# Seven block products in place of eight in sixteen FFN blocks of a decoder layer, and a down product by pairs

## The chip, the cores and the metric

One core of one Trainium2 chip runs one launch of the kernel. The metric is the time of a launch in microseconds (us), the median of three runs. Times in the trace are from one further execution, taken with the hardware profiler; durations of single instructions are in us or, where a view gives a mean, in ns. Engines are called PE (TensorE), DVE (VectorE), ACT (ScalarE), POOL (GpSimd) and SP (SyncE, which issues most loads).

## The reference, cut to what matters

One layer of a hybrid decoder, 1024 prompt tokens and 64 sample tokens (8 sequences of 8), all fp32. A token-mixing sub-layer (short convolution and three kinds of attention) comes first, then a dense SwiGLU FFN and a last RMSNorm:

```python
D_MODEL = 1024
D_FF = -(-8 * D_MODEL // (3 * 256)) * 256        # 2816

def swiglu(h, w_gate_up, w_down):
    gate, up = jnp.split(h @ w_gate_up, 2, axis=-1)
    return (jax.nn.silu(gate) * up) @ w_down
...
    x = x + gate1 * (mix @ w_out)
    x = x + gate2 * swiglu(rmsnorm(x, g_ffn) * (1 + scale2) + shift2, w_gate_up, w_down)
```

The change touches `swiglu` and a little of what stands behind it. The scales and gates are one column for all prompt tokens and one for each of the eight sample sequences.

## The kernel before

Activations lie with channels on the 128 partitions and the 1088 tokens along the free axis. `GRP` cuts the tokens into three groups of 366, 366 and 356 columns; the last holds the 64 sample tokens, so that 292 of its columns are prompt. The 2816 hidden channels are 22 FFN blocks of 128. A block needs 8 chunks of 128 input channels for its gate and 8 for its up product.

An fp32 product is made of three matmuls for each chunk (`mm3`, L197 to L204): every operand is held as a rounded half and the rest (hi and lo), and w_hi a_hi, w_hi a_lo and w_lo a_hi are added up in PSUM. A weight tile is 128x512 (four chunks); `load` (L93) brings it on SP's queue into one of five `wraw` buffers, and `halves` (L83) makes hi on ACT (L88) and lo on DVE (L89) into one of four `wsp` buffers. In an earlier part of the kernel every second L89 is on POOL (`state["sub"]`); in the FFN none is.

`gate_up` (L826) runs `gemm` twice: for the gate (two weight tiles; ACT takes Silu from PSUM into a row `u`, L829) and for the up product (two more; DVE multiplies `u` by PSUM, L833). `split_hid` then makes the halves of the hidden row, ACT L848 for hi and DVE L849 for lo. With three groups a block has 2 x 3 x 8 x 3 = 144 matmuls.

`down` (L851) multiplies hidden blocks by rows of w_down into PSUM; `add_gated` adds the result, times the gate, to the residual `x1` (DVE L760; for the third group L764 and L765 as well, for the sample tokens). `FF_GROUPS` says which blocks pass the down product together: blocks 0 to 3, then the pair (20, 21), then 4 to 7, 8 to 11, 12 to 15 and 16 to 19. For each of eight output chunks m and each token group a set of four blocks has 12 matmuls and one `add_gated`, a pair 6 and one.

Blocks 0 to 3 have groups 0 and 1 done ahead, under the attention of the sample tokens, and 20 and 21 have theirs done in front of the FFN. What the FFN itself starts with is group 2 of blocks 0 to 3 and their down product, group 2 of blocks 20 and 21 and the down product of that pair; then come the sixteen full blocks 4 to 19. The last set (16 to 19) passes the down product by other column groups, `LAST` (416, 416 and 256 columns), so that behind each of them `rstd` and the final norm follow: squares on ACT, their sums on DVE and POOL (L791), two small sets of matmuls (L794 and L798), a multiply per chunk on DVE (L970) or POOL (L968) and a store.

The order on each engine is set by the tile framework, which puts instructions in place by a timeline of its own, within what pools and buffers allow. Every engine then runs its row in order. PSUM has buffers under four tags, g (three in `gemm`), s, t and o; in the FFN of the kernel before only g is used until the last norm.

In the DRAM copies that go along with the FFN (cache outputs), `next_copy` issues one or two per block from ACT's queue.

## Time and profile before

| | us |
|---|---|
| median of three runs | 1426.48 (1424.07 to 1427.05) |
| the profiled execution, its own time | 1429.4 |
| its span, first to last instruction | 1427.6 |
| PE busy in the span | 1383.2 (97%) |
| DVE, ACT, POOL busy | 650.8, 529.3, 222.7 |
| the full blocks 4 to 19, first to last matmul of gate and up | about 835 to 1362 |
| last down product and last norm | 1363 to 1427.6 |

Busy times of PE are of matmuls whose ends are modelled, and which overlap; what one matmul costs is read from how many start in a stretch. The profiled execution took 2.9 us longer than the median, and sums are made against it.

### The profile page before, as it was taken

To read this page: it belongs to the slowest core of one execution; us is meant where nothing else is said; L and a number is where in the kernel's file an instruction comes from. 1 tells how busy PE (TensorE), PEld (TensorE's weight loads), DVE (VectorE), ACT (ScalarE), POOL (GpSimd) and SP (SyncE) were. 2 spreads that over 40 slices of the span, in tenths; PEclk is the share of its full clock that TensorE was granted. 3 is DMA by queue.
4 is the path that set the end of the run, shared out by engine and by line. 5 is a ranking of instruction groups with operands and counts; after the bars stand their busy time and mean duration, and the time that the engine had idled before them with its cause. 6 is when DMAs were issued, how large, how long until landed. Compare 5 with 4: busy or idle time off the path is not lost.

```text
span 1427.6 us, 23603 instructions
## 1 busy us (share of the span) xinstructions
PE 1383.2 (97%) x9289; PEld 1319.7 (92%) x9289; DVE 650.8 (46%) x1599; ACT 529.3 (37%) x1108; POOL 222.7 (16%) x284
## 2 busy tenths in 40 slices
PE   7999999999999999998999999999999999999996
PEld 5889999988898887888999999999999999999996
DVE  4457777255775326224554642242224222422145
ACT  5387765465654335322344312211221122112242
POOL 2143333233334220111110000000000000000023
PEclk9999999999999998999999999999999999999998
DMA  9342331352416679865444434723341332111103
GB/s 357 105 157 98 126 105 24 127 194 89 141 31 216 220 257 332 300 211 164 120 128 126 126 102 159 242 82 104 102 162 46 103 104 73 45 45 45 45 8 126
DMA packets 100799, 190.78 MB, mean 134 GB/s; under 512 B 14048, under 2 KB 51456, under 8 KB 100096
## 3 DMA queue, kind: packets, MB, share of 16 engines
q1 hardware_dynamic: 94112, 135.67, 29.8%
q10 hardware_dynamic: 6416, 53.55, 10.6%
q8 instruction: 73, 1.20, 0.3%
q14 instruction: 38, 0.31, 0.1%
q0 software_dynamic: 160, 0.04, 0.0%
HBM read 181.22 MB, written 59.23 MB: 168 GB/s over the span
## 4 chain that ended last, share of the span: by engine, by line
PE 88%; DMA 6%; DVE 2%; issue 2%; ACT 1%; POOL 1%; SPq 0%; ACTq 0%; POOLq 0%; DVEq 0%
PE ps_g L202 25%; PE ps_g L203 25%; PE ps_g L204 25%; PE ps_o L576 3%; PE ps_t L567 2%; DMA raw<-in_bv 2%; PE ps_s L525 1%; PE ps_g L178 1%; DMA wraw<-in_w_gu 1%; PE ps_s L526 1%; DMA raw<-in_bk 1%; DMA mraw<-in_wmod 1%; PE ps_s L658 1%; PE ps_o L692 1%; DMA wraw<-in_wmod 0%
## 5 line engine op out<-in xcount | busy, mean ns | idle before, releaser
L202 PE MATMUL ps_g<-act,wsp 128*128 128x366 f32 (+1 forms) x1704 | 568.4, 334 | 5.0 <-ACT wsp L88 2.6
L203 PE MATMUL ps_g<-act,wsp 128*128 128x366 f32 (+1 forms) x1704 | 565.8, 332 | 0.5 <-DVE act L614 0.5
L204 PE MATMUL ps_g<-act,wsp 128*128 128x366 f32 (+1 forms) x1704 | 564.3, 332 | 0.4 <-POOL wsp L89 0.4
L202 PEld LDWEIGHTS ps_g<-act,wsp 128*128 128x128 f32 x1704 | 323.6, 190 | 12.5 <-issue 5.5
L203 PEld LDWEIGHTS ps_g<-act,wsp 128*128 128x128 f32 x1704 | 323.8, 190 | 4.3 <-issue 2.8
L204 PEld LDWEIGHTS ps_g<-act,wsp 128*128 128x128 f32 x1704 | 322.9, 190 | 4.7 <-issue 3.3
L88 ACT ACTIVATE wsp<-wraw 128x512 fp32r<-128x512 f32 x228 | 143.1, 630 | 470.5 <-PE ps_g L204 314.5
L89 DVE TENSOR_TENSOR wsp<-wraw,wsp 128x512 fp32r<-128x512 f32 x190 | 134.4, 707 | 356.3 <-ACT wsp L88 353.5
L204 PE MATMUL ps_g<-hid,wsp 128*128 128x366 f32 (+3 forms) x416 | 136.5, 328 | 0.0
L203 PE MATMUL ps_g<-hid,wsp 128*128 128x366 f32 (+3 forms) x416 | 136.0, 327 | 0.0
L202 PE MATMUL ps_g<-hid,wsp 128*128 128x366 f32 (+3 forms) x416 | 135.6, 328 | 0.2 <-DVE ts L764 0.2
L791 POOL TENSOR_TENSOR lacc<-lacc,tmp 128x416 f32<-128x416 f32 x9 | 9.8, 1087 | 637.8 <-ACT tmp L790 637.3
L202 PEld LDWEIGHTS ps_g<-hid,wsp 128*128 128x128 f32 x416 | 78.1, 188 | 0.5 <-PE ps_g L204 0.5
L203 PEld LDWEIGHTS ps_g<-hid,wsp 128*128 128x128 f32 x416 | 78.2, 188 | 0.0
L204 PEld LDWEIGHTS ps_g<-hid,wsp 128*128 128x128 f32 x416 | 78.2, 188 | 0.0
L89 POOL TENSOR_TENSOR wsp<-wraw,wsp 128x512 fp32r<-128x512 f32 x38 | 49.6, 1306 | 166.5 <-ACT wsp L88 154.9
L539 ACT ACTIVATE Sb<-Sb,st 128x257 f32<-128x257 f32 (+5 forms) x96 | 60.6, 633 | 17.0 <-DVE st L531 15.0
L571 DVE TENSOR_TENSOR PT<-ps_t,PT 128x512 fp32r<-128x512 f32 (+1 forms) x84 | 52.2, 636 | 15.9 <-ACT PT L570 15.6
L576 PE MATMUL ps_o<-PT,Vt 128*128 128x256 f32 (+1 forms) x348 | 59.2, 288 | 0.0
L760 DVE SCALAR_TENSOR_TENSOR p_qc<-ps_g,MOD,p_qc 128x366 f32<-128x366 f32 (+3 forms) x63 | 36.0, 573 | 49.5 <-PE ps_g L204 49.2
L567 PE MATMUL ps_t<-ident,Sb 128*128 128x128 f32 x306 | 51.9, 283 | 5.9 <-DVE Sb L542 5.3
L576 PEld LDWEIGHTS ps_o<-PT,Vt 128*128 128x128 f32 x348 | 52.3, 195 | 5.1 <-issue 2.1
(319 smaller groups left out, 1604.3 us busy)
## 6 DMA issues: line engine op xcount, KB each, us to landing
wraw<-in_w_gu SPq DMA_DIRECT2D x112, 256.0 KB, 2.6
wraw<-in_wmod SPq DMA_DIRECT2D x64, 256.0 KB, 3.6
raw<-in_bk SPq DMA_DIRECT2D x30, 512.0 KB, 7.5
raw<-in_bv SPq DMA_DIRECT2D x30, 512.0 KB, 8.8
wraw<-in_w_dn SPq DMA_DIRECT2D x48, 256.0 KB, 2.7
out_bk_b<-in_bk ACTq DMA_DIRECT2D x12, 1016.0 KB, 8.8
wraw<-in_w_in SPq DMA_DIRECT2D x36, 256.0 KB, 3.1
mraw<-in_wmod SPq DMA_DIRECT2D x32, 256.0 KB, 5.7
```

What stands on the lines that cost most here:

```text
L88: S.activation(sp[:, 0, :], raw, AF.Copy)
L89: (V if not state["sub"] or state["n"] % state["sub"] else G).tensor_tensor(sp[:, 1, :], raw, sp[:, 0, :].bitcast(F32), op=OP.subtract)
L178: ins = PE.matmul(ps[32 * q:32 * q + 32, :256], lhsT=csil[:, 4 * hf + q, :], rhs=raws[2 * hf + q // 2][:, q % 2 * 256:q % 2 * 256 + 256], ...
L202: PE.matmul(ps[:, :n], lhsT=w_hi, rhs=a(0, ak), start=first and j == 0, stop=False)
L203: PE.matmul(ps[:, :n], lhsT=w_hi, rhs=a(1, ak), start=False, stop=False)
L204: PE.matmul(ps[:, :n], lhsT=w_lo, rhs=a(0, ak), start=False, stop=last and j == m - 1)
L525: PE.matmul(ps[:, :sn], lhsT=QH[:, qsl], rhs=KS[hd][:, kk], start=True, stop=False)
L539: S.activation(Sb[:, :ne], Sb[:, :ne], AF.Exp, scale=-1.0, bias=m, accum_out=st[:, 3:4])
L567: PE.transpose(pt[:, col:col + 128], Sb[:, (kb - k0) * 128:(kb - k0 + 1) * 128], ident)
L571: V.tensor_tensor(PT[:, 1, :col], pt[:, :col], PT[:, 0, :col].bitcast(F32), op=OP.subtract)
L576: PE.matmul(po[:, q0:q0 + w], lhsT=Vt[:, kb, hd].rearrange("p a b -> p (a b)"), rhs=PT[:, hl, c0:c0 + w], start=fresh, stop=ch is chunks[- ...
L760: ins = V.scalar_tensor_tensor(x1[m][:, c0:c0 + k], ps[:, :k], MOD[:, gate + m, 0:1], x1[m][:, c0:c0 + k], op0=OP.mult, op1=OP.add)
```

## The change

Sixteen full blocks (4 to 19) take the gate and up products of token groups 0 and 1 together. Seen as a 2x2 matter, the two halves of the input channels by the two products (gate, up) on the one side, and the two token groups by the two halves on the other, this is eight block products of 12 matmuls each. The new `gate_up_2x2` makes them from seven, in the form of Strassen and Winograd, of sums of weights and sums of activations. The third token group (356 columns) is done as before, with its four block products of 12.

- Weights: t1 to t4 are made on POOL, four `tensor_tensor` of 128x512 per block, into four `tw` buffers; `halves` runs on eight tiles per block (b11, t2, t3, b21, t1, t4, b22, b12) where it ran on four.
- Activations: `sums_step(k)` for k = 0 to 3 makes SA1 to SA4 once, among the third-group work of blocks 0 to 3. Each step has four POOL adds of 128x366 (`whole`: hi plus lo gives fp32), four DVE sums, four ACT copies and four DVE subtractions (`keep`). SA3 takes the place of `h2[1]` chunks 0 to 3.
- PSUM: products run under tags s and t, and three of them add to a bank that DVE or ACT has read before (`more`). Per block DVE adds PSUM to the rows `u2` and `u3` four times and into g1 once, and multiplies in SBUF for groups 0 and 1; ACT copies the first product to `u2` and takes Silu of g1 in SBUF.
- Down: `FF_GROUPS` has pairs for blocks 4 to 19, weights come as `w_d2`, `hid` has two buffers rather than five. The last pair (18, 19) alone is left for `LAST`, with four weight tiles and 144 matmuls where there were eight tiles and 288.
- Pools: tiles that are used only ahead of the FFN go to a pool `early`, closed before it. The FFN's pools have `reuse_waits="tile"`. Cache copies are issued once a block.

```diff
-FF_GROUPS = ((0, 4), (20, 2), (4, 4), (8, 4), (12, 4), (16, 4))
+FF_GROUPS = ((0, 4), (20, 2)) + tuple((f, 2) for f in range(4, 20, 2))
...
-            return ff.tile([128, 2, T], F32R, tag="hid", bufs=5, name="hid")
+            return ff.tile([128, 2, T], F32R, tag="hid", bufs=2, name="hid")
...
+        def whole(src, k):
+            t = tw()[:, :N2]
+            G.tensor_tensor(t, src[:, 0, k, :].bitcast(F32), src[:, 1, k, :].bitcast(F32), op=OP.add)
+            return t
...
+        def sums_step(k):
+
+            a21, a22, a11 = whole(h2[1], k), whole(h2[1], k + 4), whole(h2[0], k)
+            V.tensor_tensor(a22, a21, a22, op=OP.add)
+            keep(1, k, a22)
+            V.tensor_tensor(a21, a11, a21, op=OP.subtract)
+            keep(3, k, a21)
+            V.tensor_tensor(a11, a22, a11, op=OP.subtract)
+            keep(2, k, a11)
+            a12 = whole(h2[0], k + 4)
+            V.tensor_tensor(a12, a12, a11, op=OP.subtract)
+            keep(4, k, a12)
...
+        def gate_up_2x2(f, hh):
+            c2, n2 = GRP[2]
+            b11, b12, b22, b21 = [load(d["w_gu"][f, n, hf]) for n, hf in ((0, 0), (1, 0), (1, 1), (0, 1))]
+            t1, t2, t3, t4 = [tw() for _ in range(4)]
+            G.tensor_tensor(t1, b12, b11, op=OP.subtract)
+            G.tensor_tensor(t2, b22, t1, op=OP.subtract)
+            G.tensor_tensor(t3, b22, b12, op=OP.subtract)
+            G.tensor_tensor(t4, b21, t2, op=OP.subtract)
...
+            product(pa, w, lambda hl, k: h2[0][:, hl, k, :], True)
+            S.activation(u2, pa[:, :N2], AF.Copy)
+            third(pg, w, 0, True)
+            pb = ps_tile("t")
+            product(pb, wsel(halves(t2)), lambda hl, k: SA[2][:, hl, k, :], True)
+            V.tensor_tensor(u2, u2, pb[:, :N2], op=OP.add)
...
+            product(pd, wsel(halves(t4)), lambda hl, k: h2[1][:, hl, 4 + k, :], False)
+            V.tensor_tensor(g1, u2, pd[:, :N2], op=OP.add)
+            S.activation(g1, g1, AF.Silu)
+            V.tensor_tensor(g1, g1, u3, op=OP.mult)
+            split_hid(u, hh, N2, N2)
+            w = wsel(halves(b22))
+            product(pe, w, lambda hl, k: SA[4][:, hl, k, :], False)
+            V.tensor_tensor(u2, u2, pe[:, :N2], op=OP.add)
+            V.tensor_tensor(g0, g0, u2, op=OP.mult)
+            split_hid(u, hh, 0, N2)
+            ph = ps_tile("g")
+            third(ph, w, 1, True)
+            third(ph, wsel(halves(b12)), 0, False)
+            V.tensor_tensor(g2, g2, ph[:, :n2], op=OP.mult)
+            split_hid(u, hh, c2, n2)
+            next_copy(ins)
```

In the rows of the order below a line is the one in that kernel's own file: L83 to L91 of before are three lines further on in after (L91 is `halves` on DVE, L852 the hid subtraction, L836 the up multiply, L763 `add_gated`, L794 the sum of squares, L1071 the last multiply on POOL).

DVE where the FFN starts, group 2 of blocks 0 and 1, before:

```order
L89 TENSOR_TENSOR wsp<-wraw,wsp 128x512 x4
L833 TENSOR_TENSOR u<-u,ps_g 128x356
L89 TENSOR_TENSOR wsp<-wraw,wsp 128x512
L849 TENSOR_TENSOR hid<-u,hid 128x356
L89 TENSOR_TENSOR wsp<-wraw,wsp 128x512 x3
```

The same place after (`tw` holds fp32 sums, `sa_8244` to `sa_8246` and `act` their halves):

```order
L836 TENSOR_TENSOR u<-u,ps_g 128x356
L953 TENSOR_TENSOR sa_8246<-tw,sa_8246 128x366
L958 TENSOR_TENSOR tw<-tw 128x366
L91 TENSOR_TENSOR wsp<-wraw,wsp 128x512
L1032 TENSOR_TENSOR hid<-u,hid 128x356
L960 TENSOR_TENSOR tw<-tw 128x366
L91 TENSOR_TENSOR wsp<-wraw,wsp 128x512
L953 TENSOR_TENSOR sa_8244<-tw,sa_8244 128x366
L962 TENSOR_TENSOR tw<-tw 128x366
L953 TENSOR_TENSOR act<-tw,act 128x366
L91 TENSOR_TENSOR wsp<-wraw,wsp 128x512
L965 TENSOR_TENSOR tw<-tw 128x366
```

The eight sum instructions of each step stand between the halves of weights that PE's third-group matmuls wait for; all four steps stand from the last matmuls of blocks 20 and 21 ahead of the FFN to the third group of block 3, within 213 matmuls of PE's row.

DVE where the last full block of a set ends and its down product begins, before:

```order
L833 TENSOR_TENSOR u<-u,ps_g 128x366
L849 TENSOR_TENSOR hid<-u,hid 128x366
L833 TENSOR_TENSOR u<-u,ps_g 128x356
L89 TENSOR_TENSOR wsp<-wraw,wsp 128x512
L849 TENSOR_TENSOR hid<-u,hid 128x356
L760 SCALAR_TENSOR_TENSOR cv<-ps_g,MOD,cv 128x366 x2
L760 SCALAR_TENSOR_TENSOR cv<-ps_g,MOD,cv 128x292
```

The same place of a pair after (`uv` holds u2 and u3):

```order
L1007 TENSOR_TENSOR u<-uv,ps_s 128x366
L91 TENSOR_TENSOR wsp<-wraw,wsp 128x512
L1009 TENSOR_TENSOR u<-u,uv 128x366
L852 TENSOR_TENSOR hid<-u,hid 128x366
L1013 TENSOR_TENSOR uv<-uv,ps_t 128x366
L1014 TENSOR_TENSOR u<-u,uv 128x366
L91 TENSOR_TENSOR wsp<-wraw,wsp 128x512
L852 TENSOR_TENSOR hid<-u,hid 128x366
L1019 TENSOR_TENSOR u<-u,ps_g 128x356
L91 TENSOR_TENSOR wsp<-wraw,wsp 128x512
L763 SCALAR_TENSOR_TENSOR cv<-ps_g,MOD,cv 128x366
L852 TENSOR_TENSOR hid<-u,hid 128x356
```

The hidden halves of three groups now come from one run of dependent instructions in the block's last 36 matmuls, with three weight halves in it; before, those of groups 0 and 1 came 12 matmuls apart. Eight pairs pass this place where four sets did. On PE the down matmuls of a pair stand among the first five products of the next pair.

POOL from the last instruction of the second norm on, before:

```order
L824 TENSOR_TENSOR act<-tmp,act 128x64 x8
L786 MEMSET lacc 128x96
L791 TENSOR_TENSOR lacc<-lacc,tmp 128x416 x4
L786 MEMSET lacc 128x96
L791 TENSOR_TENSOR lacc<-lacc,tmp 128x416 x3
```

The same place after:

```order
L827 TENSOR_TENSOR act<-tmp,act 128x64 x8
L947 TENSOR_TENSOR tw<-act 128x366 x16
L972 TENSOR_TENSOR tw<-wraw 128x512
L973 TENSOR_TENSOR tw<-wraw,tw 128x512
L974 TENSOR_TENSOR tw<-wraw 128x512
L975 TENSOR_TENSOR tw<-wraw,tw 128x512
```

The last four rows come sixteen times, once a block, ahead of the sums of the last norm. They wait for `tw` buffers, which DVE's lo halves of the block before set free, and for `wraw` tiles from SP's queue; for a pair's first block these loads are issued behind the three weight halves in the piece of DVE's row above.

## Rows read from the trace of the kernel before

**Rows 1.** The page: busy time by engine, PE and POOL in 40 slices (tenths) of the span, and the chain of work that ended last by engine.

```profile
PE 1383.2 (97%) x9289; PEld 1319.7 (92%) x9289; DVE 650.8 (46%) x1599; ACT 529.3 (37%) x1108; POOL 222.7 (16%) x284
...
PE   7999999999999999998999999999999999999996
...
POOL 2143333233334220111110000000000000000023
...
PE 88%; DMA 6%; DVE 2%; issue 2%; ACT 1%; POOL 1%; SPq 0%; ACTq 0%; POOLq 0%; DVEq 0%
```

**Rows 2.** Busy time by stretch: start and end, length, then for each engine us busy and instructions started, the granted clock, DMA share and GB/s. The stretches are the third group of blocks 0 to 3, eight us of it, eight us in the down product of the pair (20, 21), and the sixteen full blocks up to 1330 us.

```profile
742.00:779.00 37.00, 37.00 (x228) 37.00 (x227) 15.85 (x26) 13.52 (x24) 0.44 (x2) 1.00 0.48 144
...
758.00:766.00 8.00, 8.00 (x51) 8.00 (x50) 3.73 (x6) 3.49 (x7) 0.00 (x0) 1.00 0.45 132
...
820.00:828.00 8.00, 8.00 (x50) 8.00 (x49) 6.10 (x15) 0.63 (x1) 0.00 (x0) 1.00 0.19 61
...
836.00:1330.00 494.00, 494.00 (x2976) 494.00 (x2975) 148.70 (x288) 92.64 (x169) 0.00 (x0) 1.00 0.32 102
```

**Rows 3.** Groups of instructions from 836 to 1330 us, shapes apart: busy us and mean ns of one, then idle time of the engine before them and what ended it. First the matmuls by shape (one of the three lines of each), then DVE and ACT.

```profile
L203 PE MATMUL ps_g<-act,wsp 128*128 128x366 f32 x470 | 155.2, 330 | 0.0
...
L203 PE MATMUL ps_g<-act,wsp 128*128 128x356 f32 x234 | 76.0, 325 | 0.0
...
L203 PE MATMUL ps_g<-hid,wsp 128*128 128x366 f32 x192 | 63.1, 329 | 0.0
L89 DVE TENSOR_TENSOR wsp<-wraw,wsp 128x512 fp32r<-128x512 f32 x83 | 57.5, 692 | 231.5 <-ACT wsp L88 230.8
...
L88 ACT ACTIVATE wsp<-wraw 128x512 fp32r<-128x512 f32 x82 | 51.8, 632 | 284.9 <-PE ps_g L204 205.5 <-issue 75.4 <-ACT u L829 4.0
...
L203 PE MATMUL ps_g<-hid,wsp 128*128 128x356 f32 x96 | 30.9, 322 | 0.0
L849 DVE TENSOR_TENSOR hid<-u,hid 128x366 fp32r<-128x366 f32 x28 | 15.2, 541 | 16.2 <-ACT hid L848 16.2
L833 DVE TENSOR_TENSOR u<-u,ps_g 128x366 f32<-128x366 f32 x28 | 15.0, 536 | 14.1 <-PE ps_g L204 14.1
...
L760 DVE SCALAR_TENSOR_TENSOR p_qc<-ps_g,MOD,p_qc 128x366 f32<-128x366 f32 x18 | 10.8, 599 | 17.2 <-PE ps_g L204 17.2
```

**Rows 4.** Groups on POOL over the whole span, shapes apart: a subtraction of 128x512, and an add of 128x366.

```profile
L89 POOL TENSOR_TENSOR wsp<-wraw,wsp 128x512 fp32r<-128x512 f32 x38 | 49.6, 1306 | 166.5 <-ACT wsp L88 154.9 <-issue 9.0 <-PE ps_s L526 1.6
...
L791 POOL TENSOR_TENSOR free<-free 128x366 f32<-128x366 f32 x10 | 9.2, 917 | 21.6 <-ACT free L790 21.6
```

**Rows 5.** The timeline at five places ahead of the FFN and one in the last norm: start, duration, engine and instruction. Rows of POOL and DVE that run at the same time stand together.

```profile
323.54 1.28 POOL L89 TENSOR_TENSOR wsp<-wraw,wsp 128x512 fp32r<-128x512 f32 x1
324.09 1.27 DVE L89 TENSOR_TENSOR wsp<-wraw,wsp 128x512 fp32r<-128x512 f32 x1
...
434.15 1.27 POOL L89 TENSOR_TENSOR wsp<-wraw,wsp 128x512 fp32r<-128x512 f32 x1
434.21 1.61 DVE L614 TENSOR_TENSOR act<-cv,act 128x366 fp32r<-128x366 f32 x1
...
619.07 1.27 POOL L89 TENSOR_TENSOR wsp<-wraw,wsp 128x512 fp32r<-128x512 f32 x1 [25.90 <-ACT wsp L88]
619.43 1.31 DVE L849 TENSOR_TENSOR act<-u_ff,act 128x366 fp32r<-128x366 f32 x1 [7.92 <-ACT act L848]
...
693.13 0.96 POOL L791 TENSOR_TENSOR acc<-acc,tmp 128x356 f32<-128x356 f32 x1 [24.00 <-ACT tmp L790]
693.67 0.97 DVE L89 TENSOR_TENSOR wsp<-wraw,wsp 128x512 fp32r<-128x512 f32 x1 [1.15 <-ACT wsp L88]
...
1400.76 1.08 POOL L791 TENSOR_TENSOR lacc<-lacc,tmp 128x416 f32<-128x416 f32 x1 [1.27 <-ACT tmp L790]
1400.88 0.42 DVE L760 SCALAR_TENSOR_TENSOR cv<-ps_g,MOD,cv 128x192 f32<-128x192 f32 x1 [0.28 <-PE ps_g L204]
...
1401.46 0.47 DVE L765 TENSOR_TENSOR cv<-cv,ts 128x64 f32<-128x64 f32 x1
...
1402.90 0.22 DVE L765 TENSOR_TENSOR cv<-cv,ts 128x64 f32<-128x64 f32 x1
```

**Rows 6.** The raw weight tile `wraw` from 836 to 1400 us: time from issue to landing, least, median and longest.

```profile
DMA to landing us min/median/max: 2.4/2.6/14.0
```

**Rows 7.** Busy time by stretch from the first `LAST` column group to the end (columns as in rows 2), then the timeline at the end of the last norm: the last down matmul, the small matmuls of the last two column groups (L798) and the last store.

```profile
1363.00:1390.00 27.00, 27.00 (x148) 26.81 (x147) 10.44 (x22) 10.23 (x18) 5.60 (x6) 1.00 0.00 1
1390.00:1412.00 22.00, 22.00 (x161) 21.89 (x161) 14.26 (x45) 9.35 (x20) 7.54 (x7) 1.00 0.21 78
1412.00:1428.00 16.00, 2.93 (x15) 2.36 (x13) 7.17 (x19) 1.92 (x5) 7.42 (x8) 0.61 0.50 173
...
1411.52 0.28 PE L204 MATMUL ps_g<-hid,act 128*128 128x256 f32 x1
1411.64 1.05 PE L798 MATMUL ps_s<-ident,ir_y 128*128 128x128 f32 x8
...
1419.12 1.22 PE L798 MATMUL ps_s<-ident,ir_y 128*128 128x128 f32 x4 [2.35 <-DVE ir_y L237]
...
1422.92 0.92 SPq L971 DMA_DIRECT2D out_yT<-p_qc  x2
```

More of the change, by code (lines that the diff above doesn't have):

```diff
@@ L195, in mod_tile, with mm3 @@
                                 op0=OP.add)
-    def mm3(ps, sp, kcs, a, n, first=True, last=True):
+    def mm3(ps, sp, kcs, a, n, first=True, last=True, more=False):
+        kw = dict(skip_group_check=True) if more else {}
         m = len(kcs)
@@ L201, in mm3 @@
             w_hi, w_lo = sp(0, wk), sp(1, wk)
-            PE.matmul(ps[:, :n], lhsT=w_hi, rhs=a(0, ak), start=first and j == 0, stop=False)
-            PE.matmul(ps[:, :n], lhsT=w_hi, rhs=a(1, ak), start=False, stop=False)
-            PE.matmul(ps[:, :n], lhsT=w_lo, rhs=a(0, ak), start=False, stop=last and j == m - 1)
+            PE.matmul(ps[:, :n], lhsT=w_hi, rhs=a(0, ak), start=first and j == 0, stop=False, **kw)
+            PE.matmul(ps[:, :n], lhsT=w_hi, rhs=a(1, ak), start=False, stop=False, **kw)
+            PE.matmul(ps[:, :n], lhsT=w_lo, rhs=a(0, ak), start=False, stop=last and j == m - 1, **kw)
     def wsel(sp):
@@ L865, in down_steps @@
         for q in range(4):
-            w = wsel(split(d["w_dl"][q]))
+            w = wsel(split(d["w_d2"][f0 // 2 - 2, q]))
             for m in range(2 * q, 2 * q + 2):
@@ L930, in _build @@
         for f0, nf in FF_GROUPS[:1]:
-            hid = []
+            held = [hid_tile() for _ in range(2)]
+            part = [held[f // 2][:, :, f % 2 * n2:f % 2 * n2 + n2] for f in range(4)]
             for f in range(nf):
-                hh = hid_tile()
-                gate_up(f0 + f, row("u"), hh, (2,))
-                hid.append(hh)
-            down_all(f0, hid, (2,))
+                u = row("u")
+                gate_up(f0 + f, u, None, (2,))
+                S.activation(part[f][:, 0, :], u[:, c2:], AF.Copy)
+                V.tensor_tensor(part[f][:, 1, :], u[:, c2:], part[f][:, 0, :].bitcast(F32), op=OP.subtract)
+                sums_step(f)
@@ L937, in _build @@
+            for m in range(KC):
+                ps = ps_tile("g")
+                mm3(ps, wsel(split(d["w_dn"][f0 // 4, m])), [(k, k) for k in range(4)],
+                    lambda hl, k: part[k][:, hl, :], n2)
+                add_gated(m, GRP[2], ps, 40)
         for f0, nf in FF_GROUPS[1:]:
@@ L939, in _build @@
             for f in range(f0, f0 + nf):
+                hh = hid_tile()
                 if FE <= f < FE + NPRE:
[L941 removed]
+                    u = first[f - FE]
                     split_hid(u, hh, 0, GRP[2][0])
@@ L944, in _build @@
                 else:
-                    u, hh = row("u"), hid_tile()
-                    gate_up(f, u, hh, range(3))
+                    gate_up_2x2(f, hh)
                 hid.append(hh)
@@ L949, in _build @@
                 down_all(f0, hid, range(3))
-        flat = act_tile().rearrange("p h k c -> p (h k c)")
+        sums.close()
+        fin = sums.enter_context(tc.tile_pool(name="fin", bufs=1, reuse_waits="tile"))
+        scratch["ff"] = fin
         ws = []
-        for m in range(KC):
-            sp = None if m < SPB else flat[:, (m - SPB) * 1024:(m - SPB) * 1024 + 1024].rearrange(
-                "p (h c) -> p h c", h=2)
-            ws.append(wsel(split(d["w_dn"][f0 // 4, m], sp=sp)))
+        for q in range(4):
+            w = wsel(split(d["w_d2"][f0 // 2 - 2, q]))
+            ws += [lambda hl, k, w=w, x=x: w(hl, 2 * x + k) for x in range(2)]
         for g, (c0, n) in enumerate(LAST):
@@ L971, in _build @@
                 (SP if k % 2 else S).dma_start(d["yT"][k][:, c0:c0 + n], y)
+        sums.close()
     assert not state["copies"]
```

67 lines of the change are left out of this document (51 added, 16 removed).

## The prediction, made before the changed kernel was run

> **What bounds the kernel now.** I read the page first, then the stretches, then the groups of one stretch, then the timeline where two engines meet. The page says that PE is busy for 1383.2 of 1427.6 us and makes up 88% of the chain that ended last; POOL is empty over most of the last half of the span [rows 1]. In the sixteen full blocks PE never stops: 2976 matmuls start in 494.00 us at granted clock 1.00, its 2.4 GHz level, so one costs 0.1660 us [rows 2]. Two thirds of them have 366 columns and the rest 356 [rows 3], 362.7 in the mean; one of 366 costs 0.1660 x 366 / 362.7 = 0.1675 us. In the same stretch DVE is busy for 148.70 us (30%), ACT for 92.64, POOL for none [rows 2]. So a matmul that is gone there is time gone, as long as the engines that feed PE keep ahead of it; the question is whether they still do.
>
> **Matmuls removed.** Each of 16 blocks has seven products of 12 in place of eight: 16 x 12 = 192 fewer matmuls, all of 366 columns, and PE's row of the changed kernel is shorter by just these. 192 x 0.1675 = **-32.2 us**. The down product of these blocks keeps its columns; passing it in pairs costs PE nothing.
>
> **Work added that lies beside PE.** A pair of blocks is now 2 x 84 + 2 x 48 + 144 = 408 matmuls, 67.7 us. For DVE it holds 16 weight halves for the products at 0.692 (11.1 us), ten adds of PSUM and four multiplies in SBUF at about 0.54 and two third-group multiplies (8.6), six hidden halves (3.2) [rows 3], and a pair's down product, of which the pair (20, 21) shows DVE busy 6.10 of 8.00 us [rows 2], over 24 us 18.3. Together 41 us, 61%. ACT has 20 halves at 0.632 and some 14 operations of about 0.5, 20 us [rows 3]. POOL has eight sums of 128x512; the nearest row is the subtraction of that shape, 1306 ns in the mean, 1.28 where it ran undisturbed [rows 4, 5]: 10.2 us. None is near 67.7 us, so on average all of it is hidden, and I cost it at nothing. What can cost is where it falls.
>
> **POOL and DVE shut each other out.** At 323.54 POOL starts a subtraction and DVE, at 324.09, one that takes 0.69 elsewhere; it takes 1.27 and ends 0.54 after POOL's end. At 434.15, 619.07 and 693.13 it is the same: 1.61, 1.31 and 0.97 us for operations of 0.54, 0.54 and 0.69 us by the groups [rows 3]. But L760, with one operand in PSUM, takes 0.42 beside POOL at 1400.88, while L765, both operands in SBUF, takes 0.47 where the next one takes 0.22 [rows 5]. So DVE's work on two SBUF operands waits for the rest of POOL's instruction; its PSUM adds don't. The changed kernel puts 16 POOL adds and 64 POOL sums where POOL was idle, and DVE's weight halves, hidden halves and SBUF multiplies are of the kind that waits. The Trainium skill, page "SBUF — State Buffer", section "SBUF: two separate sides", speaks against this change in the same sense: VectorE and GpSimd share a port pair as an exclusive lock, which whoever starts first keeps for the whole instruction, a VectorE operation with two SBUF inputs among them. The trace agrees, with 1.27 us for 0.69 [rows 5]. If instructions that overlap merely shared, the next two terms would be near nothing and the time about 1399; by the lock they stand as they are worked out below.
>
> **Activation sums.** Third-group work of blocks 0 to 3 has 228 matmuls in 37.00 us, 0.162 each, so 48 of a block take 7.8 us, in which DVE is busy 3.73 [rows 2]. A sums step adds eight DVE operations of 0.541 [rows 3], 8.1 us in all: that alone would just fail to fit and could be shifted. POOL's four adds are 0.917 each at that shape [rows 4], 3.7 us; shut out from the 7.6 us of DVE work on SBUF operands they make 11.3 us. In the order the four steps stand within 213 matmuls, 34.6 us, against 4 x 11.3 = 45: 10 too much, less a lead of some 24 matmuls (4 us), since weights are split up to four tiles ahead. I take **+6 us**. Lower end 0: POOL's adds fall where DVE waits for PE anyway. Upper end 12: no lead, and POOL waits too.
>
> **Passing from a pair's second block to its down product.** In the order, the last 36 matmuls of the block stand between the end of product t4 and the first down matmuls. DVE must in that time do the add to g1, a multiply, hidden lo of group 1, the add and multiply of group 0, its lo, the third multiply, and three weight halves. From the durations of rows 3, with ACT's Silu and copies between, hidden lo of group 0 is there 6.2 us after t4's end, and needed 47 matmuls after it, 7.8 us; further on the least lead is that of the first down product's `add_gated`, 0.7 us. So without POOL nothing is late. But the loads for the next pair's sums are issued behind the same weight halves and land 2.6 us later (median) [rows 6], so that POOL's t1 and t2 start within this run. Two sums that DVE meets cost up to 2 x 1.28, less the part that falls into its waits and less the lead of 0.7: 1.5 us a pair. Behind the waiting DVE instruction stand the halves that free `hid` for PE and the adds that free PSUM, so PE stops. Seven pairs have a next pair: **+10.5 us**. Lower end 0 (the sums land beside the PSUM adds), upper end 3 a pair, three sums met, 21. At the end of a pair's first block more products follow, which cover it: nothing.
>
> **Tail.** The matmuls of blocks 16 and 17's down product leave the last column groups; PE's sum is the same. But in front of the last norm's sums PE now works half as long: 49 us in the two stretches before, in which DVE was busy 24.7 and POOL 13.1 [rows 7], become some 24. DVE has then as much to do as there is time, in a fixed order, with POOL's adds beside it. The lower end is 1 us. The upper end is one whole chain of sums, small matmuls and root laid open, as it lies open behind the last down matmul, from 1411.52 to 1419.12 [rows 7]: 8 with what is queued behind it. Between them **+4.5 us**.
>
> **Sum.** -32.2 + 6 + 10.5 + 4.5 = -11.2. The profiled execution took 1429.4 us, 2.9 more than the median of the runs; 1429.4 - 11.2 = 1418.2 there, and **1415** on the footing of the median. With every lower end it is -31, or 1395; with every upper end +9, or 1435.
>
> **Rivals.**
> *All cover holds.* The added work fits on every engine on average, PE runs through, and the time is 1395 to 1406 us. For it: 61% on DVE, weights split well ahead, sums that can slip into waits. Against it: rows 5, and a least lead of 0.7 us at a place where a POOL sum takes 1.28. Chance 0.27.
> *The pass to the down product takes all four sums.* If POOL's four sums stand one after the other against DVE's run there, 4 x 1.28 - 0.7 = 4.5 us a pair, 31 us in seven, and -32.2 + 31 + 6 + 4.5 = +9: about 1436, slower than before. It decides from (32.2 - 6 - 4.5) / 7 = 3.1 us a pair on, that is when three sums are met. For it: t1 to t4 depend on one another and on loads issued together. Against it: the fourth load is issued behind the third weight half, so t4 comes later. Chance 0.15.
> *Weights come late.* A block needs four raw tiles at the same time of the five there are, so the next loads wait for its halves. The order gives each load 95 matmuls or more, 15.7 us, before PE needs what is made of it; the median landing is 2.6 us, the longest 14.0, beside a cache copy [rows 6]. With 14.0 and 2.6 more for a sum and a half it would be late by 1 us, in each of 14 to 16 blocks: 1425 to 1431 with the other terms, about no change. Chance 0.06.
>
> **How the numbers follow.** A measurement of this kernel can tell about 0.2%, 2.9 us, from no change. The forecast, some of each term, holds from 1406 to 1423 with 0.46, the full cover below it 0.27: faster 0.73. Between 1423.6 and 1429.3 lies the upper edge of the forecast and late weights: 0.11. Above it 0.16, nearly all by the second rival. The range of 1395 to 1431 leaves out most of the second rival's cases and what may lie below the sum of the lower ends, together about 0.18.
>
> **What would show it.** PE's matmuls fewer by 192 and the stretch of a pair 67.7 us plus its wait. If the steps are right, PE is idle some 6 us where the sums of activations are made, with DVE's halves as the releaser, and 1 to 2 us at each of seven passes, released by hidden lo or by `add_gated`, with DVE operations of 0.54 or 0.69 that take over 1 us beside POOL's sums. The last pair's pass, with no sums beside it, should show no wait. PE without gaps there means the first rival; waits for `wraw` mean the third. It would be wrong by more if the granted clock fell below 1.00 behind such waits, or if weights summed on POOL took much longer than a subtraction of that shape.

## The result, and the profile after

| | before | after |
|---|---|---|
| median of 4 runs each, side by side | 1425.28 us (1423.78 to 1427.05) | 1411.74 us (1411.32 to 1413.09) |
| ratio, 95% interval | | 0.9906 [0.9889, 0.9923] |
| profiled execution (span) | 1429.4 us (1427.6) | 1411.32 us (1409.5) |

The kernel is 13.5 us faster; 1415 with a range of 1395 to 1431 was forecast. The page of the kernel after, the rows that answer to [rows 1]:

```profile
PE 1353.3 (96%) x9097; PEld 1286.7 (91%) x9097; DVE 841.0 (60%) x1935; ACT 582.5 (41%) x1204; POOL 329.1 (23%) x364
...
PE   7999999999999998998998999999999999999994
...
POOL 2143343233335220102015020202021111111114
```

PE has 9097 matmuls, 192 fewer. In PE's row three slices in the middle are an 8 where one was, and the last is a 4 where it was a 6. POOL's row, empty over most of the last half before, shows the new sums. (A line of the halves, L83 to L91 of before, stands two lines further on in after: L90 is the half on ACT, L91 the one on DVE.)

Executions also differ ahead of the FFN: the start of the third group of blocks 0 to 3 (its first `ps_g<-act` matmul of 128x356) stood at 747.90 before and at 744.25 after, and between 736.8 and 748.1 in all the kernels of this study. So the terms are read by stages, from three marks in each timeline: that first matmul, the first down matmul of the pair (20, 21), and the first `LAST` matmul (128x416). The end is that of the span, which is given to 0.1 us.

| kernel | start | third group of 0-3 to pair (20, 21) | from there to `LAST` | `LAST` to the end | span |
|---|---|---|---|---|---|
| before | 747.90 | 63.28 | 550.05 | 66.37 | 1427.6 |
| after | 744.25 | 69.19 | 546.91 | 49.15 | 1409.5 |
| difference | -3.65 | +5.91 | -3.14 | -17.22 | -18.1 |

Without any wait the third stretch should fall by 192 x 0.1675 = 32.2 and gain the down product of one pair (96 matmuls of 366 columns and 48 of 356, 23.9 us), which the tail loses: -8.3 there and -23.9 in the tail. It was -3.14 and -17.22, so 5.2 us are lost in the blocks and 6.7 in the tail. In sum -32.2 + 5.9 + 5.2 + 6.7 = -14.4, which is the -18.1 without the -3.65 ahead of the third group. The medians of the runs differ by 13.5.

Where PE waited, after, from 640 us to the end (us in total, times, longest):

```profile
PE ps_s L801 <- DVE ir_y L240: 7.7, 2, 5.3
PE ps_g L207 <- DVE wsp L91: 3.9, 3, 2.4
...
PE ps_g L205 <- DVE ts L767: 3.6, 2, 3.5
...
PE ps_g L206 <- DVE hid L852: 1.7, 1, 1.7
...
PE ps_g L205 <- DVE cv L763: 0.9, 3, 0.4
```

In this order: tail (L801), sums of activations (L207), tail (L767), passes to the down product (L206 and L763). All five are released by DVE, none by a `wraw` load. The row left out between them is one wait for a load of `in_bv` at 643 us, far ahead of the FFN: 3.8 us, and 3.6 before. The same stretches as in [rows 2], after: the third group of blocks 0 to 3, two pieces at its end, a piece of the tail, the full blocks.

```profile
742.00:779.00 37.00, 33.14 (x190) 32.25 (x189) 34.03 (x54) 18.76 (x38) 16.76 (x13) 0.95 0.34 100
770.00:774.00 4.00, 3.26 (x14) 3.27 (x15) 4.00 (x10) 2.45 (x7) 0.00 (x0) 0.71 0.32 83
774.00:779.00 5.00, 5.00 (x29) 5.00 (x29) 3.85 (x7) 3.02 (x7) 0.00 (x0) 0.89 0.64 196
1386.60:1392.00 5.40, 5.28 (x32) 5.11 (x32) 4.25 (x19) 2.52 (x8) 0.91 (x1) 0.73 0.46 171
877.00:1350.00 473.00, 470.33 (x2821) 467.41 (x2820) 297.64 (x569) 131.14 (x233) 75.34 (x56) 1.00 0.30 101
```

While the sums of activations are made, DVE is busy for 34.03 of 37 us (15.85 before), and PE starts 190 matmuls in place of 228. In the blocks DVE is at 63%, close to the 61% of the prediction, and PE stops all the same. The longest wait of the sums, 2.42 us at 770.74, begins with POOL:

```profile
762.67 5.13 POOL L947 TENSOR_TENSOR tw<-act 128x366 f32<-128x366 f32 x3 [3.08 <-DVE tw L962]
766.90 1.29 DVE L958 TENSOR_TENSOR tw<-tw 128x366 f32<-128x366 f32 x1 [1.82 <-POOL tw L947]
```

The first of these three adds takes 3.25 us where the two behind it take 0.99 and 0.97; beside it DVE's operations on SBUF run one behind the other up to 765.08. DVE then stands idle for 1.82 us, because its sum needs the second add, and the weight halves behind that sum come late.

A pass to the down product that lost most, the first one of the run, timeline of PE, DVE and POOL after (start, duration):

```profile
876.69 0.53 DVE L1009 TENSOR_TENSOR u<-u,uv 128x366 f32<-128x366 f32 x1
...
879.72 1.29 POOL L972 TENSOR_TENSOR tw<-wraw 128x512 f32<-128x512 f32 x1 [26.81 <-DMA wraw<-in_w_gu]
879.80 1.61 DVE L1014 TENSOR_TENSOR u<-u,uv 128x366 f32<-128x366 f32 x1
...
881.09 1.48 POOL L973 TENSOR_TENSOR tw<-wraw,tw 128x512 f32<-128x512 f32 x1
881.33 1.78 DVE L91 TENSOR_TENSOR wsp<-wraw,wsp 128x512 fp32r<-128x512 f32 x1
...
882.53 1.71 POOL L974 TENSOR_TENSOR tw<-wraw 128x512 f32<-128x512 f32 x1
...
883.04 1.59 DVE L852 TENSOR_TENSOR hid<-u,hid 128x366 fp32r<-128x366 f32 x1
...
884.69 0.44 PE L206 MATMUL ps_g<-hid,wsp 128*128 128x366 f32 x1 [1.71 <-DVE hid L852]
```

Three operations of 0.54, 0.69 and 0.54 us take 1.61, 1.78 and 1.59, each beside one POOL sum; the hidden lo of group 0 (L852) is the last of them, and PE waits for it. And a pass that lost nothing:

```profile
1082.83 0.53 DVE L1009 TENSOR_TENSOR u<-u,uv 128x366 f32<-128x366 f32 x1
...
1085.94 0.54 DVE L1014 TENSOR_TENSOR u<-u,uv 128x366 f32<-128x366 f32 x1
...
1087.06 0.54 DVE L852 TENSOR_TENSOR hid<-u,hid 128x366 fp32r<-128x366 f32 x1
...
1088.19 0.69 DVE L91 TENSOR_TENSOR wsp<-wraw,wsp 128x512 fp32r<-128x512 f32 x1 [0.15 <-ACT wsp L90]
1088.27 1.77 POOL L972 TENSOR_TENSOR tw<-wraw 128x512 f32<-128x512 f32 x1 [29.25 <-DMA wraw<-in_w_gu]
1088.99 0.60 DVE L763 SCALAR_TENSOR_TENSOR cv<-ps_g,MOD,cv 128x366 f32<-128x366 f32 x1
```

Here the load landed later, and POOL's first sum starts 5.44 us behind L1009 where it was 3.03 above. DVE's last half of the run had begun 0.08 us earlier: now POOL is the one that waits (1.77 for 1.29). The adds of PSUM that follow take their usual time.

The tail's 6.7 us, by the timeline after (DVE, PE):

```profile
1382.99 1.19 DVE L1073 SCALAR_TENSOR_TENSOR cv<-cv,gT,ps_s 128x416 f32<-128x416 f32 x2
...
1384.11 1.75 DVE L1073 SCALAR_TENSOR_TENSOR p_qc<-p_qc,gT,ps_s 128x416 f32<-128x416 f32 x3
...
1386.28 0.21 DVE L767 TENSOR_TENSOR ts<-ps_g,MOD 128x64 f32<-128x64 f32 x1
...
1386.64 0.55 PE L205 MATMUL ps_g<-hid,wsp 128*128 128x256 f32 x1 [3.46 <-DVE ts L767]
...
1391.64 0.28 PE L207 MATMUL ps_g<-hid,wsp 128*128 128x256 f32 x1
```

PE waits 3.46 us for an add out of PSUM that stands behind five multiplies by the norm of an earlier column group (2.9 us). These multiplies take their usual 0.6 us each: this is DVE's order, not a collision with POOL. Then the granted clock is 0.73 up to the last down matmul: 0.27 x 5.40 = 1.5 (an estimate from the granted clock). From the first `LAST` matmul to the last down matmul it was 1411.52 - 1361.23 = 50.29 us before [rows 7] and is 1391.64 - 1360.35 = 31.29, which is 19.0 less where 23.9 were due: 4.9, the sum of these two. From there to the small matmuls of the last root it was 1419.12 - 1411.52 = 7.60 [rows 7] and is 1401.26 - 1391.64 = 9.62: 2.0 more (the rows stand in the last section). From there to the end it is 0.2 less.

### The profile page after: what moved, and what is told of

Its sections match the earlier page's. It is cut to its first block, busy times and chain, and to the rows that moved or that the text cites. A ratio compares the mean times of both kernels' runs of the same rounds, so it can differ in the third digit from the quotient of the medians.

```text
span 1409.5 us, 23915 instructions
## 1 busy us (share of the span) xinstructions
PE 1353.3 (96%) x9097; PEld 1286.7 (91%) x9097; DVE 841.0 (60%) x1935; ACT 582.5 (41%) x1204; POOL 329.1 (23%) x364
## 4 chain that ended last, share of the span: by engine, by line
PE 83%; DMA 7%; DVE 4%; issue 2%; POOL 1%; ACT 1%; SPq 0%; POOLq 0%; ACTq 0%; DVEq 0%
PE ps_g L205 18%; PE ps_g L207 18%; PE ps_g L206 18%; PE ps_s L206 3%; PE ps_s L205 3%; PE ps_s L207 3%; DMA wraw<-in_w_gu 3%; PE ps_o L579 3%; PE ps_t L206 2%; PE ps_t L205 2%; PE ps_t L207 2%; PE ps_t L570 2%; DMA raw<-in_bv 1%; PE ps_g L180 1%; PE ps_s L528 1%
## 5 line engine op out<-in xcount | busy, mean ns | idle before, releaser
L205 PE MATMUL ps_g<-act,wsp 128*128 128x366 f32 (+1 forms) x1192 | 400.0, 337 | 5.5 <-ACT wsp L90 3.3
L207 PE MATMUL ps_g<-act,wsp 128*128 128x366 f32 (+1 forms) x1192 | 396.0, 333 | 4.0 <-DVE wsp L91 3.9
L206 PE MATMUL ps_g<-act,wsp 128*128 128x366 f32 (+1 forms) x1192 | 397.7, 334 | 0.4 <-DVE act L617 0.4
L90 ACT ACTIVATE wsp<-wraw 128x512 fp32r<-128x512 f32 x232 | 145.3, 629 | 270.5 <-PE ps_g L207 170.4
L205 PEld LDWEIGHTS ps_g<-act,wsp 128*128 128x128 f32 x1192 | 227.6, 191 | 13.0 <-issue 5.5
L207 PEld LDWEIGHTS ps_g<-act,wsp 128*128 128x128 f32 x1192 | 227.1, 191 | 9.2 <-DVE wsp L91 5.0
L91 DVE TENSOR_TENSOR wsp<-wraw,wsp 128x512 fp32r<-128x512 f32 x194 | 144.5, 745 | 146.3 <-ACT wsp L90 141.5
L206 PEld LDWEIGHTS ps_g<-act,wsp 128*128 128x128 f32 x1192 | 227.8, 191 | 4.0 <-issue 2.5
L205 PE MATMUL ps_g<-hid,wsp 128*128 128x366 f32 (+3 forms) x464 | 152.7, 331 | 4.6 <-DVE ts L767 3.6
L206 PE MATMUL ps_g<-hid,wsp 128*128 128x366 f32 (+3 forms) x464 | 152.3, 328 | 1.7 <-DVE hid L852 1.7
L207 PE MATMUL ps_g<-hid,wsp 128*128 128x366 f32 (+3 forms) x464 | 152.6, 329 | 0.0
L972 POOL TENSOR_TENSOR tw<-wraw 128x512 f32<-128x512 f32 x16 | 21.8, 1365 | 322.9 <-DMA wraw<-in_w_gu 157.0
L205 PEld LDWEIGHTS ps_g<-hid,wsp 128*128 128x128 f32 x464 | 87.6, 189 | 7.2 <-issue 3.6
L90 ACT ACTIVATE wsp<-tw 128x512 fp32r<-128x512 f32 x64 | 40.5, 633 | 122.5 <-PE ps_g L207 59.3
L206 PE MATMUL ps_s<-act,wsp 128*128 128x366 f32 x272 | 90.2, 332 | 0.0
L205 PE MATMUL ps_s<-act,wsp 128*128 128x366 f32 x272 | 90.1, 331 | 0.0
L206 PEld LDWEIGHTS ps_g<-hid,wsp 128*128 128x128 f32 x464 | 87.9, 189 | 2.5 <-DVE hid L852 2.3
L207 PE MATMUL ps_s<-act,wsp 128*128 128x366 f32 x272 | 89.9, 330 | 0.0
L91 POOL TENSOR_TENSOR wsp<-wraw,wsp 128x512 fp32r<-128x512 f32 x38 | 49.9, 1313 | 169.6 <-ACT wsp L90 158.0
L207 PEld LDWEIGHTS ps_g<-hid,wsp 128*128 128x128 f32 x464 | 87.8, 189 | 0.0
L763 DVE SCALAR_TENSOR_TENSOR p_qc<-ps_g,MOD,p_qc 128x366 f32<-128x366 f32 (+3 forms) x99 | 56.5, 572 | 39.9 <-PE ps_g L207 38.0
L763 DVE SCALAR_TENSOR_TENSOR p_q<-ps_g,MOD,p_q 128x366 f32<-128x366 f32 (+3 forms) x99 | 55.3, 570 | 38.5 <-PE ps_g L207 38.5
```

Of the source, the lines that this page charges most:

```text
L90: S.activation(sp[:, 0, :], raw, AF.Copy)
L91: (V if not state["sub"] or state["n"] % state["sub"] else G).tensor_tensor(sp[:, 1, :], raw, sp[:, 0, :].bitcast(F32), op=OP.subtract)
L205: PE.matmul(ps[:, :n], lhsT=w_hi, rhs=a(0, ak), start=first and j == 0, stop=False, **kw)
L206: PE.matmul(ps[:, :n], lhsT=w_hi, rhs=a(1, ak), start=False, stop=False, **kw)
L207: PE.matmul(ps[:, :n], lhsT=w_lo, rhs=a(0, ak), start=False, stop=last and j == m - 1, **kw)
L763: ins = V.scalar_tensor_tensor(x1[m][:, c0:c0 + k], ps[:, :k], MOD[:, gate + m, 0:1], x1[m][:, c0:c0 + k], op0=OP.mult, op1=OP.add)
```

## The experiments

Theory at the start: all three losses are one mechanism; POOL's instruction and DVE's work on two SBUF operands shut each other out, at places where DVE's run was just short enough. Rivals: DVE has simply too much to do there, whoever makes the sums; or the sums make weights late. A pair's period is taken from one L1009 of a pair's second block to the next; 67.7 us is a period without loss, 408 x 0.1660.

**The sums of activations on DVE**, and POOL's four adds of a step gone:

```
-            G.tensor_tensor(t, src[:, 0, k, :].bitcast(F32), src[:, 1, k, :].bitcast(F32), op=OP.add)
+            V.tensor_tensor(t, src[:, 0, k, :].bitcast(F32), src[:, 1, k, :].bitcast(F32), op=OP.add)
```

> The 16 adds of activation halves (366 columns) go from POOL to DVE; the rest as in the changed kernel. There the third group of blocks 0 to 3 took 37.6 us against 31.4 before. Theory, DVE and POOL shut each other out: without POOL in that stage DVE needs 8.1 + 4 x 0.54 = 10.3 us a step in place of about 11.3 and the gaps between them; over the 34.6 us of matmuls that is 41, less 4 of lead, a wait of 2.6 in place of 6.2: the stage takes about 34 us, the time is about 1408. Rival, DVE simply has too much to do there and POOL does no harm: DVE gets 8.7 us more work, and the stage takes 42 to 46 us, the time is 1416 to 1420.

Median 1403.02 us (1395.95 to 1410.43), ratio to before 0.9854 [0.9822, 0.9886]. The stage took 63.09 us, where before took 63.28: the whole loss is gone, more than the theory gave. (Of the 8.7 us between this median and that of after, 6.1 are this stage; the rest lies within the scatter of this kernel's runs.) Windows of this kernel and its group of weight halves from 742 to 779 us, and the same group after:

```profile
742.00:779.00 37.00, 37.00 (x227) 36.72 (x225) 32.51 (x68) 19.44 (x40) 0.00 (x0) 1.00 0.40 121
```
```profile
L91 DVE TENSOR_TENSOR wsp<-wraw,wsp 128x512 fp32r<-128x512 f32 x17 | 11.7, 686 | 0.8 <-ACT wsp L90 0.8
```
```profile
L91 DVE TENSOR_TENSOR wsp<-wraw,wsp 128x512 fp32r<-128x512 f32 x15 | 12.5, 836 | 0.0
```

In this window DVE has twelve of the sixteen adds more and is busy for less time, 32.51 in place of 34.03. The windows don't hold quite the same work; from 8 us ahead of the third group to the pair (20, 21), DVE starts 122 instructions in 57.40 us of busy time, where after has 106 in 58.45. So it was not too much work: POOL's help cost DVE as much as the adds themselves, in operations that took longer, and 3.9 us of idle time for POOL's results on top (L958, one of the two waits is shown above). The experiment takes away both; it doesn't tell them apart. The periods kept their losses (70.73, 67.71, 67.70, 67.86, 67.71, 68.50, 68.40).

**The sums of weights on DVE** (`t1` to `t4`):

```
-            G.tensor_tensor(t1, b12, b11, op=OP.subtract)
+            V.tensor_tensor(t1, b12, b11, op=OP.subtract)
...
```

> The 64 weight sums go from POOL to DVE, all else as in the changed kernel. No POOL instruction is then left in the full blocks, and DVE has 5.5 us more of 67.7 a pair. In DVE's row three of the sums stand within the pass, ahead of the last hidden half and the first add of the down product, and the first of them waits for loads that land about 5.2 us after L1009. Theory, what counts is what stands in DVE's run at the pass: 2.1 us of sums and about 1 us for the load less 0.7 of lead make 2 to 3 us a pass, seven times, in place of 5.2 in all: 1421 to 1428. Rival, only POOL's lock costs there: all periods 67.7 us, 1406.

Median 1426.99 (1417.40 to 1433.95), 1.0004 [0.9979, 1.0028]. Every period lost 1.7 to 4.0 us (69.67, 70.07, 69.42, 70.03, 69.86, 69.99, 71.66), 16.7 in all, as the theory had it: DVE's run at the pass is the tight place, and each sum of 0.69 in it costs, together with DVE's wait for the load in front of the first one (0.56 us in the pass at 1010.21). The 71.66 holds besides some 3 us in which matmuls of 366 columns came 0.305 us apart, behind a wait of 1.35 us at 1299.0. PE's waits in that kernel:

```profile
PE ps_g L205 <- DVE cv L763: 9.1, 7, 1.4
...
PE ps_g L206 <- DVE hid L852: 1.6, 5, 0.5
```

**The sums of weights held back behind the whole run.** A POOL copy of one column of the last hidden lo stands ahead of `t1`, in every block:

```
+            ins = G.tensor_copy(mark, prev[:, 1, T - 1:T].bitcast(F32))
+            with tc.issue_after(ins.ins):
...
```

> A small POOL copy that reads the last hidden half of the block before stands ahead of each block's weight sums, so that POOL's four sums start behind the pass to the down product in place of within it; DVE's row at the passes is the same. In the changed kernel four of seven passes cost 3.0, 0.85, 0.87 and 0.52 us over a clean pair of 67.71. Theory, POOL's sums hold up DVE there: all seven periods of a pair are 67.7 to 67.8 us, time 1406 to 1407, unless sums that start later make weight halves late. Rival, DVE's own run of dependent instructions is too long and POOL does no harm: the periods keep their 5.2 us in all, 1411 to 1412.

Median 1433.76, 1.0057 [1.0036, 1.0078]; both expectations missed. Each period was 71.6 us, 3.9 too long, the last pair's too. The waits for `hid` and `cv` were gone, and others stood in their place:

```profile
PE ps_t L205 <- ACT wsp L90: 10.3, 8, 1.3
...
PE ps_t L207 <- DVE wsp L91: 4.1, 8, 0.5
```

`ps_t` is the product of `t2`: at the change of blocks inside a pair its sums came too late for it. These waits take some 2.1 us of a pair; behind them the granted clock was 0.62 from 1008.5 to 1013.0 us in one pair, with matmuls of 366 columns 0.305 us apart, and this makes up most of the other 1.8. So there is no room to hold the sums back in every block.

**The sums of activations spread over the stretch**, still on POOL: step 0 ahead of the third group, steps 1 and 2 behind blocks 0 and 2, step 3 in the down product of these blocks, steps 1 to 3 each behind a small POOL copy.

```
-                sums_step(f)
+                if f in (0, 2):
+                    sums_step(1 + f // 2, u[:, T - 1:T])
...
+            sums_step(3, x1[7][:, T - 1:T])
```

> The same activation sums, on the same engines, in another place: step 0 first, steps 1 and 2 behind the third group of blocks 0 and 2, step 3 behind the down product of blocks 0 to 3, held there by a small POOL copy. PE's row is the same. Theory, in that stage DVE and POOL together need more time than the matmuls give: with the work spread over 69 us of matmuls (11.3 + 3.8 us a step against 15 or more) the stage's wait goes from 6.2 to 0 to 2 us, time 1406 to 1408. Rival, the wait comes from the ACT copies or the loads of that stage, not from the crowding: no change, 1411 to 1412.

Median 1405.60 (1402.56 to 1409.68), 0.9868 [0.9847, 0.9889]. The stage took 63.61 us, PE without a gap, with DVE at 26.09 of 31 us:

```profile
748.00:779.00 31.00, 31.00 (x192) 31.00 (x191) 26.09 (x39) 15.86 (x31) 10.88 (x10) 1.00 0.44 127
```

So the loss was one of density, as the prediction's sum for that stage had it, and either less of it on POOL or more room takes it away.

**Each sum of weights made twice on POOL**, 10 us more of POOL's work in a pair:

```
+            for t, x, y in ((t1, b12, b11), (t2, b22, t1), (t3, b22, b12), (t4, b21, t2)):
+                for _ in range(2):
+                    G.tensor_tensor(t, x, y, op=OP.subtract)
```

> Each of the 64 weight sums is made twice by POOL, the second time over the same result; nothing else changes. POOL is then busy 20 of 67.7 us of a pair in place of 10. Theory, a DVE instruction that meets a POOL sum waits for it, and a pass has 0.7 us of lead: each of seven passes costs 1.3 to 3 us more, time 1420 to 1432. Rival, the sums are hidden beside PE as their average says: within 1.5 us of 1411.7.

Median 1413.31 (1407.50 to 1416.65), 0.9910 [0.9888, 0.9932]: the theory's number failed. The rival's was missed by 0.1 us, which the runs can't tell from a hit. The periods were 72.34, 67.70, 67.71, 67.70, 67.71, 67.71 and 68.31. Twice the work cost nothing in five of seven pairs. So it isn't how much POOL adds but whether its first sums start within DVE's run. Over the 35 passes of the five profiles with the sums on POOL at the time the load lands (after, and the experiments 1, 4, 5 and the tail below), by the start of the first sum behind L1009:

| first sum starts | passes | period above 67.7 |
|---|---|---|
| 2.9 to 3.1 us | 5 | 3.0 to 4.6 |
| 4.9 to 5.3 us | 10 | 0.52 to 0.88 |
| 5.4 us or later | 20 | 0 to 0.15 |

The run's last half (L91) starts 5.36 us behind L1009; that is where the edge lies. The five early ones are the first pass of each of the five executions. Their spread has a second cause: the two at 3.0 (after, experiment 1) kept a granted clock of 1.00, while the three at 3.7 to 4.6 show one of 0.57 to 0.66 over 4 or 5 us behind PE's wait.

**Held back at the pass alone.** The copy ahead of `t1` reads the last product's row `u`, which L1019 and L1027 write, and stands only in a pair's first block:

```
+            if f % 2 == 0 and "u" in last:
...
+                mark = G.tensor_copy(mark, last["u"][:, T - 1:T])
+            with tc.issue_after(mark.ins) if mark is not None else ExitStack():
...
```

> As the changed kernel, but the weight sums of a pair's first block stand behind a small POOL copy that reads the third-group row of the block before, so that the first sum can start no earlier than 5.4 us after the multiply of group 1's hidden row in that pass (L1009). Over 28 passes of four runs a sum that started 5.4 us or more after it cost nothing, one at 4.9 to 5.3 cost 0.5 to 0.9 us, and the first pass of each run, with sums from 3 us on, cost 3.0 to 4.6. Theory, a sum costs only what it takes from DVE's run of weight and hidden halves there: all seven periods 67.7 us, 5.2 us less, time about 1406.5. Rival, what costs is the late start of sums as in the run with the copy behind the last hidden half (71.6 us a pair): waits for the half of t2, 1411 or more.

Median 1404.05 (1401.44 to 1405.63), 0.9845 [0.9816, 0.9875]. All seven periods were 67.70 to 67.71, and the third stretch 541.64 us, within 0.2 of 550.05 - 8.3. The first pass of this kernel, and PE in the window shown above of after (470.33 of 473.00 there, 31 matmuls fewer):

```profile
877.48 0.53 DVE L1017 TENSOR_TENSOR u<-u,uv 128x366 f32<-128x366 f32 x1
...
882.75 0.19 POOL L977 COPY mark<-u 128x1 f32<-128x1 f32 x1 [28.95 <-DVE u L1027]
882.84 0.69 DVE L91 TENSOR_TENSOR wsp<-wraw,wsp 128x512 fp32r<-128x512 f32 x1 [0.16 <-ACT wsp L90]
882.92 1.77 POOL L979 TENSOR_TENSOR tw<-wraw 128x512 f32<-128x512 f32 x1
```
```profile
877.00:1350.00 473.00, 473.00 (x2852) 473.00 (x2852) 297.97 (x573) 133.07 (x237) 76.44 (x64) 1.00 0.31 103
```

With nothing but the start of the sums moved, by 2.4 us at the first pass, PE doesn't stop once in 473 us. The passes' 5.2 us are this collision.

**Both**, experiment 1 and the held-back sums together:

> The copy of the run before and the activation sums on DVE together. If the two waits are apart from one another, 6.1 and 5.2 us go: stage of the third group without a wait, seven periods of 67.7 us, time 1398 to 1401. If what goes at one place comes back at the other or in the last norm: 1403 to 1406.

Median 1397.27 (1392.45 to 1399.21), 0.9798 [0.9770, 0.9827]; the three stretches 63.08, 541.65 and 49.18.

**The tail with its matmuls doubled again** (the down product of the `LAST` groups made of each weight half twice, 288 matmuls as before, so that it is counted double):

```
-                down(ws[m], m, (c0, n), hid)
+                ps = ps_tile("g")
+                mm3(ps, ws[m], [(0, 0), (1, 1)] * 2, lambda hl, k: hid[k][:, hl, c0:c0 + n], n)
+                add_gated(m, (c0, n), ps, 40)
```

> Leaves the reference: in the last column groups each pair's down product is summed twice over, so that these groups have 288 matmuls again in place of 144; everything else is as in the changed kernel. The matmuls added take 96 x 0.190 + 48 x 0.117 = 23.9 us. Theory, the last part lost 6.7 us because DVE, POOL and the root of a group have half the cover: 23.9 us of matmuls cost only about 17 us, the part from the first down matmul of these groups to the end takes 65 to 67.5 us, the time is 1428 to 1430. Rival, the 6.7 us come from the pools or weights of that part and not from the cover: 73 us, 1435 to 1436.

Median 1424.62 (1421.51 to 1428.92), 0.9995 [0.9978, 1.0011]. The tail took 65.95 us, 16.8 more than after, for 23.9 us of matmuls; so 7.1 us of that time had been lost, within 0.4 of the 6.7 above. The length was as the theory had it; the time was not, 1424.62 where 1428 to 1430 was expected, and why the other executions are shorter than the profiled one (1428.92, the longest of them) stays open. From the last down matmul to the small matmuls of the last root it is 7.60 us again, as before. PE is full again up to the last down matmuls, beside the same work on the others:

```profile
1361.15:1410.00 48.85, 48.85 (x304) 48.72 (x303) 25.03 (x64) 20.04 (x38) 13.12 (x13) 1.00 0.10 36
```

**The last multiplies later**, on top of both: the five DVE multiplies by the norm of the first column group stand behind the last sum of squares of the third.

```
+                with tc.issue_after(ins.ins):
+                    for k, y, gain, r0, n0 in late:
+                        V.scalar_tensor_tensor(y, y, gain, r0[:, :n0], op0=OP.mult, op1=OP.mult)
...
```

> As the run with both edits, and in the last part the five DVE multiplies of the first column group's norm stand behind the last sum of squares, in place of among the third group's down products, where PE waited 3.4 us for a PSUM bank behind them. Theory, DVE is what binds the last part: PE's wait of 3.4 us goes, but the root of the last group then stands behind eight multiplies in place of three, 3.3 us later: the part stays at 48 to 50 us. Rival, the wait of PE is what prolongs it: 45.5 to 46.5 us, time 1394.

Median 1393.72 (1392.73 to 1398.43), 0.9783 [0.9761, 0.9806]. The tail took 48.09 us, against 49.18. PE's waits from 1340 us on in this kernel:

```profile
PE ps_s L803 <- DVE ir_y L240: 9.0, 2, 6.0
...
PE ps_g L205 <- DVE ts L767: 1.5, 1, 1.5
```

The wait for the add out of PSUM (L767) is half of what it was (3.2 in the kernel with both), and that for the root is 2.5 longer (6.5 there). One microsecond is gained and most of it moves. The tail is where the theory had it; the time alone would fit the rival's 1394, but of the 3.2 us between the two profiled spans 2.1 lie ahead of the third group. The interval overlaps that of the kernel with both; which of the two is faster stays open. Both beat the kernel before and the changed one.

## Why the prediction was right, by its own steps

The time came out 3.3 us from the 1415, and part of that nearness is luck: the passes were 5.3 us cheaper than forecast and the tail 2.2 dearer, so two errors partly cancelled.

- **Matmuls removed, -32.2.** Right. Periods of 67.70 to 67.71 us wherever nothing waits, and the third stretch of 541.64 with the sums held back, show that all of it comes back as time.
- **Work beside PE at nothing.** Right, on average and in each place where it isn't late: the weight sums made twice cost nothing in five of seven pairs.
- **Lock between POOL and DVE.** Right, and it carries two of the three losses: DVE's operations beside sums took 1.59 to 1.78 us for 0.54 to 0.69, its adds of PSUM 0.60, and the loss went away with POOL's work (experiment 1) or with its start (held back at the pass). In the tail it has a part in the last root at most. This agrees with the Trainium skill, page "SBUF — State Buffer", section "SBUF: two separate sides": whoever starts first holds the shared pair for the whole instruction. The table of 35 passes shows what that means here: 0.1 us decide who waits.
- **Activation sums, +6 (0 to 12).** 5.9. Its size was right, its make-up not: 3.9 of it are waits, and the clock fell behind the longest of them, which the sum didn't have (last section). The upper end's "POOL waits too" did happen, in the add of 3.25 us.
- **Passes, +10.5 (0 to 21).** The mechanism was right, and this term was mis-sized: 5.2. The step that failed is the one from the median landing of the loads to 1.5 us for *each* pair. Where a collision is over or not within 0.1 us, there is no typical price: three passes lost nothing, three lost 0.5 to 0.9, and one lost 3.0. The 1.28 of a sum was right; what was missing is where in the run of 5.4 us a landing 2.6 us behind its issue falls. I had placed it inside; in most passes it falls at the very end. The lead of 0.7 us did not show either. In a pass that lost 0.88 us, L1009 at 1219.09:

```profile
1226.11 0.59 DVE L763 SCALAR_TENSOR_TENSOR cv<-ps_g,MOD,cv 128x366 f32<-128x366 f32 x1
...
1226.75 0.44 PE L205 MATMUL ps_g<-hid,wsp 128*128 128x366 f32 x1 [0.40 <-DVE cv L763]
```

The first `add_gated` starts 7.02 us behind L1009, where a clean pass has 6.16: 0.86 late, and all of it lost. In the other two of these passes it is 0.83 late for 0.86 lost, and 0.49 for 0.52.
- **Tail, +4.5 (1 to 8).** 6.7, within the bounds, but not by what the upper end was made of. The chain of the last root lay open before as well and grew by 2.0 us only. What is new is that DVE has too much to do in a fixed order, as the step said: 3.5 us of wait for one add, and 1.5 by the clock behind it, which the sum didn't have. The doubled matmuls show that what was missing is cover, matmuls beside which DVE can work; that the 2.0 are POOL's multiplies beside the root is read from the timeline and not tried.
- **Rivals.** *All cover holds* is out for this kernel, but is nearly what the kernel with both edits shows: 1397 us, inside its 1395 to 1406. *The pass takes all four sums* needed 3.1 us a pair: one pass in seven came near it. *Weights come late* is out for the changed kernel (no wait for `wraw` in the blocks). Where the sums were held back in every block, weight halves did come late, 1433.8 us, but by the copy and not by a load.

Open: why the first pass's loads land earlier than the others'. They are issued at the same distance from L1009; another cache copy (`out_bk` in place of `out_bv`) runs beside them. That was seen, not tried.

## What to carry to other kernels

Work that goes to an idle engine is not free because the averages leave room: look for what it locks, and at which places the neighbour's chain has less lead than one such instruction. Ask there *when* the new work starts, not how much of it there is; a start that one landing decides makes the price jump between nothing and its worst, so give both with their counts in place of a mean. And where POOL and DVE would share a stretch, the sum may be cheaper on the busier of the two, as the activation sums were (6.1 us gained), or on POOL behind a mark that lets DVE's run pass first. It isn't so everywhere: the weight sums on DVE cost 16.7 us in the passes, where those on POOL cost 5.2.
